# Other homes for the first operands of FFN-out in a one-core encoder layer

## The chip, the cores and the metric

The kernel runs on one core of a Trainium2 chip. The metric is the device time of one execution in microseconds; lower is better. The median of three runs before the change is 2306.59 us (2305.39 to 2307.46).

## What is computed

One layer of an encoder trunk on x of 1024 tokens by 1024 columns, in float32. It has three sub-layers, each between two RMS norms: a SwiGLU feed-forward block (FFN), a token mixing block (retention and neighbourhood attention), and a second FFN. The FFNs are what the change touches:

```python
def _swiglu(x, w_in, w_out):
    g, u = jnp.split(x @ w_in, 2, axis=-1)
    return (jax.nn.silu(g) * u) @ w_out
...
        h = _swiglu(_rms_norm(x, ffn1_pre_norm[l]), ffn1_w_in[l], ffn1_w_out[l])
        x = x + 0.5 * _rms_norm(h, ffn1_post_norm[l])
        m = _token_mixing(...)
        x = x + _rms_norm(m, mix_post_norm[l])
        h = _swiglu(_rms_norm(x, ffn2_pre_norm[l]), ffn2_w_in[l], ffn2_w_out[l])
        x = x + 0.5 * _rms_norm(h, ffn2_post_norm[l])
```

D_FF is 2816, that is 22 blocks of 128. "Layer 1" and "layer 2" below, and in the change's short description, are the first and the second FFN.

## The kernel before

**Products in three parts.** TensorE takes its operands in a reduced float format. So each float32 operand is split (`split`, L60 and L61): ScalarE casts it into a high part h, VectorE subtracts h and leaves a low part l. A product is then three matmuls, h·h, h·l and l·h (`mm3`, L87 to L89).

**Two-by-two blocks with seven products.** Both matrix products of an FFN are done as a Strassen-Winograd product: the left factor is kept as a11, a12, a22 and four sums s1 to s4, seven operands in place of eight blocks, and VectorE forms the sums of the right factor.

**FFN-in** (`ffn_in`, L404, and `Pairs.run`, L363) runs over 22 pairs, i = 0 to 21. A pair loads two raw weight tiles (tile wraw, three of 4 KB; all sizes here are per partition) and makes seven products in the order of the left operands a11, s2, a12, s3, s1, a22, s4. The left operands x (names a11h, a11l and so on, 14 tiles of 8 KB) stay in SBUF in pool a1 (layer 1) or a2 (layer 2). A pair's result is gated (SiLU at L414, product at L416) into a tile gt of 4 KB, of which there are three. After each second pair `LeftFactors` (L431) makes the left operand of FFN-out: GpSimd forms four sums (tile cmb, L441) from the halves of two gt tiles, and stores these and three unsummed halves to DRAM (tensors g0a.. and g0s.. in layer 1, g1a.. and g1s.. in layer 2). The stores are issued by GpSimd in the order of its list; a gt tile can be used anew when they have read it.

Before the 22 pairs, `Pairs.lead` (L330) makes the a11 and a12 products of the first six pairs in layer 1: three pairs stay in PSUM, three are saved in six tiles "lead" of 2 KB, which runs 3, 4 and 5 read at L376 (ScalarE) and L384 (VectorE). Beside the pairs `OutSums` (L508) prepares the right factor of FFN-out: for each of 11 column groups it loads four tiles tw (2 KB each, L517), makes four differences in place (L522) and stores them (tensors t).

**FFN-out** (`ffn_out`, L535) goes through 7 products x 11 blocks, 77 steps. A step takes a left block ("G operand") and a right block. `Blocks` (L446) loads the left block from DRAM into graw (L457, issued by SyncE), then splits it into gh and gl; the three are 2 KB each. The right block comes through wraw (L610, L614) and is split into wh and wl, of which there are eight each. A step has 12 matmuls, and operands are asked for three steps ahead. `Blocks` takes its pools in turn from a tuple of four: in layer 1 (g0, g0, g0, g1), so blocks 0, 1, 2 come from pool gl10 and block 3 from gl11, with three graw tiles in the first and one in the second; in layer 2 (g0, g1, g0, g1) with two each.

**Order and places.** Each engine works through its own list in order. The build makes the lists: it may put an instruction ahead of the program's order once its inputs and the place of its output are free. Pools are stacked in SBUF from two sides, left (upwards) and right (downwards). All pools here are opened with a rule by which a tile waits only for the tiles that had its bytes before, not for their whole pool. Between the end of the weight pool w and the right-hand edge there are 172 KB. Counted upwards from the end of w, in KB:

- layer 1, FFN-in: tw1 0 to 16; fin1 16 to 36 (two tiles each of c0 and c1 at 16 to 24, the three gt at 24 to 36); early 40 to 60 (four cmb, six lead); a1 60 to 172. Before it, norm1 had 0 to 28.
- layer 1, FFN-out: mid0 0 to 20; gl10 20 to 38 (graw 20 to 26, gh 26 to 32, gl 32 to 38); mid1 38 to 50; gl11 50 to 56; mid2 56 to 64; the rest on the right.
- layer 2, FFN-in: cmb2 0 to 8; tw2 8 to 24; fin2 24 to 44 (gt 32 to 44); a2 48 to 160; gs2 160 to 172.
- layer 2, FFN-out: out2 0 to 36; gl21 36 to 48; junk2 48 to 88; gl20 160 to 172.

Of the kernel before, what the change touches and what calls it, by code (L numbers as in the profile page):

```python
# [10 lines left out]
F32 = mybir.dt.float32  # L11
# [7 lines left out]
P = 128  # L19
# [216 lines left out]
class Winograd:  # L236
# [20 lines left out]
    def put(self, t, g, pt):  # L257
        c, nc = self.c, self.c.nc
        ts = slice((t % 4) * P, (t % 4 + 1) * P)
        if t < 4:  # L260
            c.split(*self.part(("a11", "a12")[g], ts), pt)
            return

        def tmp():
            return self.tmp.tile([P, 4, P], F32, tag="cmb", name="cmb", bufs=4)

        h1, l1 = [q.bitcast(F32) for q in self.part("a11", ts)]
        h2, l2 = [q.bitcast(F32) for q in self.part("a12", ts)]

        if g == 0:  # L270
            self.a21, self.s3 = tmp(), tmp()
            nc.scalar.copy(self.a21, pt)
            if self.spill is not None:
                c.store(self.spill[:, :, ts], self.a21)
            eng = nc.gpsimd if t in self.s3_on_pool else nc.vector
            eng.tensor_tensor(self.s3, h1, self.a21, ALU.subtract)
            eng.tensor_tensor(self.s3, self.s3, l1, ALU.add)
            return
        a21, s3 = self.a21, self.s3
        s1 = a21 if self.spill is None else tmp()  # L280
        c.split(*self.part("a22", ts), pt)
        nc.vector.tensor_tensor(s1, pt, a21, ALU.add)
        c.split(*self.part("s3", ts), s3)
        nc.vector.tensor_tensor(s3, pt, s3, ALU.subtract)
        c.split(*self.part("s1", ts), s1)
        c.split(*self.part("s2", ts), s3)
        nc.gpsimd.tensor_tensor(s3, h2, s3, ALU.subtract)  # L287
        nc.gpsimd.tensor_tensor(s3, s3, l2, ALU.add)  # L288
        return lambda: c.split(*self.part("s4", ts), s3, eng=nc.gpsimd)
# [9 lines left out]
class Pairs:  # L299
# [30 lines left out]
    def lead(self, save=None, between=(), on_pool=()):  # L330

        n = self.held + self.saved
        for i in (*range(self.held, n), *range(self.held)):
            if i in self.begun:
                continue
            g = self.c.raw(self.srcs[i][0])
            eng = self.c.nc.gpsimd if i in on_pool else None
            ps = [self.product("a11", g[:, :512], eng), self.product("a12", g[:, 512:], eng)]
            if between:
                f = between.pop(0)()  # L340
                if f is not None:
                    between.append(f)
            if i >= self.held:
                sb = [save(), save()]
                for a, b in zip(sb, ps):
                    for p, s in self.pieces(a):
                        self.c.nc.scalar.copy(p, b[:, s])
                ps = sb
            self.begun[i] = ps
# [54 lines left out]
def ffn_in(c, pairs, pool, put, sums):  # L404

    nc = c.nc
    for i in range(FT):
        gate = [pool.tile([P, 512], F32, tag=f"c{j}", name=f"c{j}", bufs=2) for j in range(2)]
        gt = pool.tile([P, S], F32, tag="gt", name="gt", bufs=3)
        up = gt[:, :512], gt[:, 512:]  # L410

        def done(j):
            if j < 2:
                nc.scalar.activation(gate[j], gate[j], AF.Silu)  # L414
            if j in (1, 2):
                e = nc.vector.tensor_tensor(up[j % 2], gate[j % 2], up[j % 2], ALU.mult)  # L416
                with c.tc.issue_after(e.ins):
                    sums(i, j)
        pairs.run(i, (*gate, *up).__getitem__, done)
        put(i, gt)  # L420
# [237 lines left out]
def stream(c, pool, src):  # L658

    def lhs(k, toks):  # L660
        n = len(toks) * P
        p0 = toks[0] * P
        raw = pool.tile([P, 384], F32, tag="graw", name="graw", bufs=2)
        h = pool.tile([P, 384], F32R, tag="gh", name="gh", bufs=3)
        l = pool.tile([P, 384], F32R, tag="gl", name="gl", bufs=3)
        c.nc.sync.dma_start(raw[:, :n], src(k)[:, p0:p0 + n])
        c.split(h[:, :n], l[:, :n], raw[:, :n])
        return {t: (h[:, j * P:(j + 1) * P], l[:, j * P:(j + 1) * P]) for j, t in enumerate(toks)}
    return lhs
# [340 lines left out]
def trunk_layer(ctx: ExitStack, tc, x, g1a, w1i, w1o, g1b, gma, wmt, wnv, wrv, logits, dtab, rope, bias,  # L1010
# [7 lines left out]
    c = Core(tc, const, wpool, psum, dram)  # L1018
# [4 lines left out]
    def dt(name, shape):  # L1023
        return dram.tile(shape, F32, name=name)

    gl = [{n: dt(f"g{i}{n}", [P, FT // 2 * 512]) for n in Winograd.NAMES} for i in range(2)]
    t1o, t2o = ([dt(f"t{i}{n}", [P, FT // 2 * 512]) for n in range(4)] for i in range(2))
# [9 lines left out]
    def rows(a):  # L1037
        return lambda t: a[t * P:(t + 1) * P, :]

    right, left = ExitStack(), ExitStack()  # L1040

    def pool(stack, name, side="left"):
        return stack.enter_context(tc.tile_pool(name=name, bufs=1, side=side, reuse_waits="tile"))
# [3 lines left out]
    early = pool(right, "early", "right")  # L1047
    wx = Winograd(c, (apool,) * 3, early, (14,) * 7)
    with tc.tile_pool(name="norm1", bufs=1, reuse_waits="tile") as ep:
        g = ep.tile([P, D], F32, tag="gpre", name="gpre", bufs=1)  # L1050
        nc.sync.dma_start(g, g1a)
        for t in range(TT):
            xt = ep.tile([P, D], F32, tag="epx", name="epx", bufs=3)
            nc.sync.dma_start(xt, x[t * P:(t + 1) * P, :])
            f = c.norm_T(xt, g, t, ep, wx.put)()
            if f is not None:
                f()
        fin = Pairs(c, wx, [(w1i[i], w1i[FT + i]) for i in LeftFactors.order], 3, 3)
        fin.lead(lambda: early.tile([P, 512], F32, tag="lead", name="lead", bufs=6), on_pool=(3, 4, 5, 0))
    with (tc.tile_pool(name="tw1", bufs=1, reuse_waits="tile") as tw,  # L1060
          tc.tile_pool(name="fin1", bufs=1, reuse_waits="tile") as fp):
        ffn_in(c, fin, fp, LeftFactors(c, early, gl[0]),
               OutSums(c, lambda: tw.tile([P, 512], F32, tag="tw", name="tw", bufs=8), w1o, t1o))
    right.close()

    x0pool = pool(right, "x0", "right")
# [2 lines left out]
    wx = Winograd(c, (x0pool, x1pool, None), None, (4, 4, 2, 8, 8, 8, 8), d["a21"])  # L1069
# [3 lines left out]
    q = [ep.tile([P, 4, 512], F32, tag="q", name="q", bufs=2) for _ in range(2)]  # L1073
# [4 lines left out]
    junk = [m0.tile([P, 512], F32, name=f"junk{u}") for u in range(2)]  # L1078
    g0 = pool(mid, "gl10")
    m1 = pool(mid, "mid1")  # L1080
    junk += [m1.tile([P, 512], F32, name=f"junk{u}") for u in range(2, 4)]
    g1, m2 = pool(mid, "gl11"), pool(mid, "mid2")
    rest = ffn_out(c, q, Blocks(c, (g0, g0, g0, g1), (3, 1)), junk,
                   lambda t: (m1, m2, ep, ep)[t // 2].tile([P, D], F32, tag="xs", name="xs", bufs=2 + t // 4 * 2),
                   w1o, t1o, gl[0], fo,
                   {n: (lambda j=j: ahead.update({j: c.load_w(wnv[j])})) for j, n in enumerate((65, 66))})
# [213 lines left out]
    cmb = pool(left, "cmb2")  # L1300
    wx = Winograd(c, (apool,) * 3, cmb, (14,) * 7)
    wx.s3_on_pool = (4, 5)
    with tc.tile_pool(name="ep2", bufs=1, reuse_waits="tile") as ep:
        rest = c.out_proj(KT, stream(c, gs, lambda k: d["m"][k]), lambda k: c.load_w(wmo[k]),
                          Ep(c, ep, gmb, g2a, False, rows(x1), rows(x2), wx.put))
        fin = Pairs(c, wx, [(w2i[i], w2i[FT + i]) for i in LeftFactors.order], 3, 1)

        def save():
            return [gs.tile([P, 384], F32, tag=n, name=n, bufs=3)[:, :256] for n in ("gh", "gl")]

        fin.lead(save, rest)
        for f in rest:
            f()


    tw = pool(left, "tw2")
# [3 lines left out]
    left.close()  # L1320
    a_stack.close()
    g_stack.close()
    g0 = pool(right, "gl20", "right")
    op = pool(left, "out2")
    q = [op.tile([P, 4, 512], F32, tag="q", name="q", bufs=4) for _ in range(4)]
    fo = Epilogue(c, op, g2b, None, rows(x2), rows(out), None)
    g1 = pool(left, "gl21")
    jp = pool(left, "junk2")
    junk = [jp.tile([P, 512], F32, name=f"junk{u}") for u in range(4)]
    ffn_out(c, q, Blocks(c, (g0, g1, g0, g1), (2, 2)), junk,  # L1330
# [81 lines left out]
```

## Time and profile before

| what | value |
|---|---|
| median of three runs | 2306.59 us |
| the profiled execution | 2306.69 us |
| its span on the core | 2304.8 us |
| granted TensorE clock, mean | 0.989 |
| ScalarE (ACT) busy | 1003.4 us, 44% |
| GpSimd (POOL) busy | 593.1 us, 26% |
| DMA | 422.63 MB, mean 183 GB/s |

The profile names the engines PE (TensorE matmul), PEld (its weight loads), DVE (VectorE), ACT (ScalarE), POOL (GpSimd) and SP (SyncE, which only issues DMAs). A row of the timeline gives start, duration, engine, line, operation, out<-in by the program's tile names, and how often; in brackets the idle time of the engine before it and what ended it. "wl<-wraw,wh" on DVE at L61 is the low part of a weight piece, "gh<-graw" on ACT at L60 the high part of a left block of FFN-out. Ends of matmuls are modelled: at full pace they start some 0.23 us apart and are shown 0.39 us long.

### The profile page before, as it was taken

The page shows a single profiled execution, that of the slowest core. Times are in us where ns is not written, and L with a number is a line of the kernel's source. Part 1 is how long each engine was busy: PE and PEld are TensorE (multiplying, and loading weights), DVE is VectorE, ACT ScalarE, POOL GpSimd, SP SyncE. Part 2 cuts the span into 40 slices and gives each one's busy share as a digit, 9 for nine tenths or more (in the row PEclk, how much of TensorE's full clock was granted, in tenths as well). Part 3 has the DMA queues.
Part 4 walks back from the last instruction along what each step waited for, and adds up shares of the span by engine and source line. Part 5 has one row for each costly group of instructions (what it writes and reads, how often), then busy time and mean ns, then how long its engine had stood idle before and what let it go on. Part 6 is the DMA issues. An engine that isn't in the chain of part 4 may idle for free.

```text
span 2304.8 us, 30361 instructions
## 1 busy us (share of the span) xinstructions
PE 2218.8 (96%) x10288; PEld 1839.6 (80%) x10288; DVE 1675.8 (73%) x2945; ACT 1003.4 (44%) x2102; POOL 593.1 (26%) x689
## 2 busy tenths in 40 slices
PE   6999999999998999999999999999799999998998
PEld 5788888778776877778888888887588888887886
DVE  7897777645778758869875688547897777774576
ACT  6333332244554322258885675225533322233453
POOL 5342423210124134411101222101534242421012
PEclk9999999999999999999999999999899999999999
DMA  5464545477654542257645577866555454546765
GB/s 177 153 205 147 178 144 176 153 231 227 207 192 142 178 165 96 110 185 238 220 161 178 163 222 235 291 213 204 173 172 187 151 173 146 174 138 213 233 199 185
DMA packets 163675, 422.63 MB, mean 183 GB/s; under 512 B 19712, under 2 KB 47488, under 8 KB 163456
## 3 DMA queue, kind: packets, MB, share of 16 engines
q1 hardware_dynamic: 130080, 310.04, 42.4%
q0 software_dynamic: 33440, 110.65, 12.4%
q8 instruction: 81, 1.33, 0.2%
q14 instruction: 74, 0.61, 0.1%
HBM read 301.60 MB, written 123.21 MB: 184 GB/s over the span
## 4 chain that ended last, share of the span: by engine, by line
PE 80%; DVE 11%; issue 3%; POOL 3%; DMA 1%; ACT 1%; SPq 0%; POOLq 0%; DVEq 0%; ACTq 0%
PE ps L89 25%; PE ps L87 24%; PE ps L88 24%; DVE wl L61 2%; PE pt L89 1%; PE pt L87 1%; PE pt L88 1%; POOL rstd L97 1%; PE ps L725 1%; PE pt L744 1%; POOL cmb L287 1%; DVE tmp L117 1%; DVE t L378 1%; POOL cmb L288 1%; DVE xs L493 1%
## 5 line engine op out<-in xcount | busy, mean ns | idle before, releaser
L61 DVE TENSOR_TENSOR wl<-wraw,wh 128x512 fp32r<-128x512 f32 x662 | 468.9, 728 | 80.4 <-ACT wh L60 79.4
L60 ACT CAST wh<-wraw 128x512 fp32r<-128x512 f32 x670 | 390.3, 618 | 218.2 <-PE ps L88 71.2
L87 PE MATMUL ps<-wh,gh 128*128 128x512 f32 x612 | 241.5, 396 | 19.2 <-ACT gh L60 18.1
L61 DVE TENSOR_TENSOR gl<-graw,gh 128x512 fp32r<-128x512 f32 (+2 forms) x178 | 124.3, 699 | 173.8 <-ACT gh L60 173.6
L88 PE MATMUL ps<-wl,gh 128*128 128x512 f32 x612 | 241.2, 395 | 2.1 <-DVE wl L61 2.1
L89 PE MATMUL ps<-wh,gl 128*128 128x512 f32 x612 | 240.1, 395 | 0.8 <-DVE gl L61 0.5
L60 ACT CAST gh<-graw 128x512 fp32r<-128x512 f32 (+2 forms) x178 | 107.1, 602 | 226.6 <-PE ps L88 87.4
L414 ACT ACTIVATE c<-c 128x512 f32<-128x512 f32 x88 | 55.7, 633 | 283.1 <-DVE c L384 198.5
L87 PEld LDWEIGHTS ps<-wh,gh 128*128 128x128 f32 x612 | 116.4, 190 | 45.9 <-ACT gh L60 19.7
L89 PEld LDWEIGHTS ps<-wh,gl 128*128 128x128 f32 x612 | 116.4, 191 | 28.2 <-DVE gl L61 4.0
L88 PEld LDWEIGHTS ps<-wl,gh 128*128 128x128 f32 x612 | 116.6, 191 | 26.8 <-DVE wl L61 3.2
L483 POOL TENSOR_TENSOR q<-q,gain 128x512 f32<-128x512 f32 x22 | 33.6, 1546 | 357.7 <-ACT ps L482 343.4
L60 ACT CAST wh<-t 128x512 fp32r<-128x512 f32 x58 | 36.1, 622 | 202.6 <-DVE t L378 184.5
L89 PE MATMUL ps<-a12h,wl 128*128 128x512 f32 x280 | 110.4, 394 | 3.7 <-DVE wl L61 3.7
L87 PE MATMUL ps<-a11h,wh 128*128 128x512 f32 x280 | 112.4, 401 | 1.4 <-ACT wh L60 0.7
L89 PE MATMUL ps<-a11h,wl 128*128 128x512 f32 x280 | 110.9, 396 | 0.7 <-DVE wl L61 0.7
L87 PE MATMUL ps<-a12h,wh 128*128 128x512 f32 x280 | 111.1, 397 | 0.0
L88 PE MATMUL ps<-a11l,wh 128*128 128x512 f32 x280 | 111.0, 397 | 0.0
L88 PE MATMUL ps<-a12l,wh 128*128 128x512 f32 x280 | 109.8, 392 | 0.0
L87 PE MATMUL ps<-a22h,wh 128*128 128x512 f32 x280 | 109.8, 392 | 0.0
L89 PE MATMUL ps<-a22h,wl 128*128 128x512 f32 x280 | 109.1, 390 | 0.0
L88 PE MATMUL ps<-a22l,wh 128*128 128x512 f32 x280 | 109.0, 389 | 0.0
(354 smaller groups left out, 5975.6 us busy)
## 6 DMA issues: line engine op xcount, KB each, us to landing
wraw<-in_dram SPq DMA_DIRECT2D x243, 512.0 KB, 4.4
tw<-in_dram SPq DMA_DIRECT2D x88, 256.0 KB, 3.3
t<-tw POOLq DMA_DIRECT2D x88, 256.0 KB, 4.2
wraw<-t SPq DMA_DIRECT2D x40, 512.0 KB, 3.6
g0s<-cmb POOLq DMA_DIRECT2D x44, 256.0 KB, 4.2
graw<-g0s SPq DMA_DIRECT2D x44, 256.0 KB, 2.8
g1s<-cmb POOLq DMA_DIRECT2D x44, 256.0 KB, 4.2
graw<-g1s SPq DMA_DIRECT2D x44, 256.0 KB, 2.7
```

What stands on the lines that cost most here:

```text
L60: nc.scalar.copy(h, src)
L61: (eng or nc.vector).tensor_tensor(l, src, hf, ALU.subtract)
L87: mm(ps, a[0], b[0], start=start, stop=False)
L88: mm(ps, a[0], b[1], start=False, stop=False)
L89: mm(ps, a[1], b[0], start=False, stop=stop)
L97: self.nc.gpsimd.tensor_tensor(r[:, :n], ms, self.mhalf[:, :n], ALU.pow)
L117: nc.vector.scalar_tensor_tensor(xn[:, bs], x[:, bs], r[:, 0:1], gain[:, bs], op0=ALU.mult, op1=ALU.mult)
L287: nc.gpsimd.tensor_tensor(s3, h2, s3, ALU.subtract)
L288: nc.gpsimd.tensor_tensor(s3, s3, l2, ALU.add)
L378: tt(t2, b22, t1, ALU.subtract)
L414: nc.scalar.activation(gate[j], gate[j], AF.Silu)
L483: (eng or c.nc.gpsimd).tensor_tensor(h if out is None else out, h, self.post[:, b * 512:(b + 1) * 512], ALU.mult)
```

## The change

In layer 1 the pool tw1 is gone: the tw tiles are taken from the same tag as the saved leads, "lead", which has eight tiles in place of six. So FFN-in of layer 1 has only fin1 on the left side, now at 0 to 20 KB, and the pool early grows to 24 KB (36 to 60). `Blocks` of layer 1 gets two graw tiles in each pool in place of three and one; gl10 is then 16 KB (20 to 36), mid1 36 to 48, gl11 48 to 56.

In layer 2 a loop calls `wx.op` for the seven left operands of FFN-in in the reverse of the order in which a pair uses them, before the products that fill them; and gl21 moves to the right side, below gl20, at 148 to 160 KB, so that junk2 begins at 36.

```diff
         fin = Pairs(c, wx, [(w1i[i], w1i[FT + i]) for i in LeftFactors.order], 3, 3)
-        fin.lead(lambda: early.tile([P, 512], F32, tag="lead", name="lead", bufs=6), on_pool=(3, 4, 5, 0))
-    with (tc.tile_pool(name="tw1", bufs=1, reuse_waits="tile") as tw,
-          tc.tile_pool(name="fin1", bufs=1, reuse_waits="tile") as fp):
-        ffn_in(c, fin, fp, LeftFactors(c, early, gl[0]),
-               OutSums(c, lambda: tw.tile([P, 512], F32, tag="tw", name="tw", bufs=8), w1o, t1o))
+
+
+        def lead():
+            return early.tile([P, 512], F32, tag="lead", name="lead", bufs=8)
+
+        fin.lead(lead, on_pool=(3, 4, 5, 0))
+    with tc.tile_pool(name="fin1", bufs=1, reuse_waits="tile") as fp:
+        ffn_in(c, fin, fp, LeftFactors(c, early, gl[0]), OutSums(c, lead, w1o, t1o))
     right.close()
...
-    rest = ffn_out(c, q, Blocks(c, (g0, g0, g0, g1), (3, 1)), junk,
+    rest = ffn_out(c, q, Blocks(c, (g0, g0, g0, g1), (2, 2)), junk,
...
     wx.s3_on_pool = (4, 5)
+    for n in ("s4", "a22", "s1", "s3", "s2", "a12", "a11"):
+        wx.op(n)
...
-    g0 = pool(right, "gl20", "right")
+    g0, g1 = pool(right, "gl20", "right"), pool(right, "gl21", "right")
     op = pool(left, "out2")
     q = [op.tile([P, 4, 512], F32, tag="q", name="q", bufs=4) for _ in range(4)]
     fo = Epilogue(c, op, g2b, None, rows(x2), rows(out), None)
-    g1 = pool(left, "gl21")
     jp = pool(left, "junk2")
```

## The prediction

> **What bounds the kernel now.** I read the page first (busy shares, slices, chain), then windows of 10 us around the two thin places of the slices, then the timeline there.
>
> ```profile
> PE 2218.8 (96%) x10288; PEld 1839.6 (80%) x10288; DVE 1675.8 (73%) x2945; ACT 1003.4 (44%) x2102; POOL 593.1 (26%) x689
> PE   6999999999998999999999999999799999998998
> PE 80%; DVE 11%; issue 3%; POOL 3%; DMA 1%; ACT 1%; SPq 0%; POOLq 0%; DVEq 0%; ACTq 0%
> ```
>
> TensorE is busy 96% of the span and carries 80% of the chain, so only its idle time and its slow time can be won. Two idle places lie where FFN-in hands over to FFN-out; call them joint 1 (layer 1) and joint 2 (layer 2). Columns: stretch, then busy us of PE, PEld, DVE, ACT, POOL, granted clock, DMA share, GB/s.
>
> ```profile
> 450.00:460.00 10.00, 6.29 (x28) 4.88 (x26) 6.97 (x11) 2.50 (x4) 2.79 (x4) 1.00 0.42 134
> 460.00:470.00 10.00, 3.84 (x9) 3.02 (x10) 1.33 (x2) 1.24 (x2) 6.80 (x9) 0.53 0.67 246
> 470.00:480.00 10.00, 10.00 (x43) 8.20 (x43) 5.33 (x9) 5.30 (x10) 0.00 (x0) 0.96 0.84 270
> 2070.00:2080.00 10.00, 8.98 (x40) 7.12 (x38) 7.53 (x12) 3.64 (x6) 2.80 (x4) 1.00 0.43 137
> 2080.00:2090.00 10.00, 3.88 (x9) 3.06 (x10) 3.46 (x4) 1.24 (x2) 7.24 (x9) 0.60 0.81 268
> 2090.00:2100.00 10.00, 10.00 (x41) 8.08 (x41) 3.88 (x6) 3.46 (x7) 0.00 (x0) 0.89 0.48 152
> ```
>
> Joint 1 in the timeline (start, duration, engine, line, tiles, and in brackets the idle time before it with its releaser):
>
> ```profile
> 455.90 0.39 PE L89 MATMUL ps<-s4h,wl 128*128 128x512 f32 x1
> 461.11 0.56 POOL L67 DMA_DIRECT2D t<-tw  x1
> 462.89 0.56 POOL L67 DMA_DIRECT2D g0a<-gt  x1
> 465.25 0.32 SPq L457 DMA_DIRECT2D graw<-g0a  x1
> 465.49 0.62 ACT L60 CAST gh<-graw 128x512 fp32r<-128x512 f32 x1 [8.72 <-DMA g0a<-gt]
> 466.16 0.80 PE L87 MATMUL ps<-wh,gh 128*128 128x512 f32 x1 [9.87 <-ACT gh L60]
> 471.19 0.39 PE L87 MATMUL ps<-wh,gh 128*128 128x512 f32 x1
> ```
>
> FFN-in's last matmul ends at 456.29. The first cast into gh (L60) stands still until the store of the last gated tile has read it: POOL issues that store only at 462.89, behind its sums. So the home of gh is a gt tile, and the pool sizes say the same: counted from the end of the weight pool, fin1's gt fills 24 to 36 KB, gl10's gh 26 to 32. PE loses 9.87 us. Then it runs slowly: the block's 12 matmuls take 466.16 to 471.19, 5.03 us. A block at full pace is the step between these two loads, 2.72 us:
>
> ```profile
> 478.02 0.32 SPq L457 DMA_DIRECT2D graw<-g0a  x1
> 480.74 0.32 SPq L457 DMA_DIRECT2D graw<-g0s  x1
> ```
>
> That is 2.31 us more. Joint 2 differs: block 0 runs at once, block 1 waits.
>
> ```profile
> 2076.10 0.39 PE L87 MATMUL ps<-wh,gh 128*128 128x512 f32 x1
> 2081.62 0.32 SPq L457 DMA_DIRECT2D graw<-g1a  x1
> 2085.45 1.25 ACT L60 CAST gh<-graw 128x512 fp32r<-128x512 f32 x2 [5.52 <-DMA graw<-g1a]
> 2086.12 0.79 PE L87 MATMUL ps<-wh,gh 128*128 128x512 f32 x1 [7.14 <-ACT gh L60]
> 2092.23 0.40 PE L89 MATMUL ps<-wh,gl 128*128 128x512 f32 x1
> ```
>
> ```profile
> SPq L457 <- POOL cmb L441: 0.7, 1, 0.7
> ```
>
> Block 1's load (pool gl21, 36 to 48 KB) lies on fin2's gt (32 to 44 KB); SP's last wait before it is for POOL's sum L441, which reads gt. PE idles 7.14 us; the 14 starts from 2086.12 to 2092.23 take 6.11 us where 14/12 x 2.72 = 3.17 would do: 2.94 more.
>
> **The change, part by part.**
>
> *Joint 1.* fin1 moves down to 0 to 20 KB; gl10 (graw 2, gh 3, gl 3 tiles of 2 KB) takes 20 to 36 KB, and the enlarged early pool begins at 36 of the 172 KB that are free. Nothing that FFN-in uses is left under blocks 0, 1 and 2. What then holds them? Only their stores and the engines' queues. Layer 2 already shows such operands:
>
> ```profile
> 1756.26 0.33 SPq L457 DMA_DIRECT2D graw<-g1a  x1
> 1760.61 0.62 ACT L60 CAST gh<-graw 128x512 fp32r<-128x512 f32 x1 [4.68 <-DMA graw<-g1a]
> 1761.26 0.69 DVE L61 TENSOR_TENSOR gl<-graw,gh 128x512 fp32r<-128x512 f32 x1 [2.34 <-ACT gh L60]
> 1760.00:1770.00 10.00, 10.00 (x46) 8.29 (x45) 7.62 (x13) 3.46 (x7) 0.00 (x0) 1.00 0.25 84
> ```
>
> This one is loaded some 320 us ahead, and the row of 2076.10 above has no idle time in brackets: PE goes from FFN-in to block 0 without a gap. So joint 1 should lose its 9.87 us, and without idle time also the slow 2.31: 12.18 us. What is late next is block 3 (pool gl11, 48 to 56 KB), now on the lead tiles, in which w_out's sums end. PE wants it at 456.29 + 3 x 2.72 = 464.45. The last of those stores is issued at 461.11 and lands 2.3 us later:
>
> ```profile
> t<-tw POOLq DMA_DIRECT2D x1, 256.0 KB, 2.3
> DMA to landing us min/median/max: 2.5/2.8/4.4
> ```
>
> That is 463.4. If gh or gl of block 3 lies there, cast and difference (0.62 + 0.69) end at 464.7: at most 0.3 lost. If graw does (one of eight tiles), a load of 2.8 (second row, graw in FFN-out) comes first: 467.5, 3.1 us lost. I take 0.
>
> *Two graw tiles for three of four blocks* (was 3 and 1). A tile is wanted again after two blocks, 5.44 us; cast, difference and load need 0.62 + 0.69 + 2.8 = 4.1, with the longest load 5.7. Casts run more than two blocks ahead of PE, which covers the 0.3. Cost 0; above, 0.3 if that cover goes.
>
> *Joint 2.* gl21 goes to the right side, 148 to 160 KB, on top of FFN-in's operands a2. There are two readings of the new loop over op(). If tiles take their place when first written, as the q tiles of the built program do (q[2], written before q[1], stands in the place that is given out earlier), the layout stays and gl21 lies on a11l and a12h. If the loop reverses it, gl21 lies on s4l and a22h. Last uses in the last pair:
>
> ```profile
> L89 PE MATMUL ps<-a12h,wl x8: 389/389/389, 2043.9 to 2065.0; 128*128 128x512 f32 x8
> L88 PE MATMUL ps<-s4l,wh x8: 389/389/389, 2054.6 to 2075.6; 128*128 128x512 f32 x8
> ```
>
> On a12h the loads start at 2065.4 and all is there 11 us early. On s4l the cast starts at 2076.0; with DVE's tail before it gl is done by 2078 to 2079.5, wanted at 2076.10 + 2.72 = 2078.82: 0 to 0.7 lost. I take 0: gain 7.14 + 2.94 = 10.08. Blocks 0 and 2 keep their pool.
>
> *The front of layer 1.* The w_out tiles tw lose their own 16 KB and share eight with the six saved leads. Two are free at once; the rest come free only as runs 3 to 5 read their leads:
>
> ```profile
> L376 ACT COPY c<-lead x3: 621/622/623, 99.2 to 128.2; 128x512 f32<-128x512 f32 x3
> L384 DVE TENSOR_TENSOR c<-lead,c x3: 676/693/1070, 117.1 to 145.3; 128x512 f32<-128x512 f32 x3
> L522 DVE TENSOR_TENSOR tw<-tw x16: 677/682/1186, 96.6 to 192.2; 128x512 f32<-128x512 f32 x16
> DMA to landing us min/median/max: 2.4/4.1/6.4
> 130.00:140.00 10.00, 9.84 (x44) 7.83 (x43) 9.97 (x13) 4.57 (x8) 7.25 (x9) 1.00 0.75 270
> ```
>
> Six of the first eight loads and their subtractions (L522, 0.68 each) move 20 to 45 us later, into a stretch where DVE is full (9.97 of 10) and PE just fed (9.84). The work is the same. Two loads may also run ahead into the first 10 us; 0.52 MB at 270 GB/s (the last row) are 1.9 us if all of it delays the start, 0 if none. PE can gain 0.16 there at most. I take half, +0.9; ends -0.2 and, if DVE waits in full, the slow rival below.
>
> *Sum.* -12.18 - 10.08 + 0.9 = -21.4 us. The profiled execution took 2306.69 us (span 2304.8), the median is 2306.59: **2285 us**. Work behind the joints follows them in fixed order with PE full, so I let the shift carry to the end.
>
> [...]
>
> **The rivals.**
>
> *Block 3's graw waits for the last tw store* (10%): -21.4 + 3.1 = 2288; with a slow restart as in joint 1, 2291. For it: one tile in eight. Against: a tile freed one pair earlier serves as well.
>
> *The order of the queues stays* (8%): block 0's home is free, but SP still loads it after the last w_out load.
>
> ```profile
> 458.03 7.53 SPq L457 DMA_DIRECT2D graw<-g0a  x2
> graw<-g0a SPq DMA_DIRECT2D x1, 256.0 KB, 4.1
> ```
>
> 458.03 + 4.1 + 0.62 = 462.8: 6.5 idle plus 2.3 slow remain, 2285 + 8.8 = 2294. Against it: the load at 1756.
>
> *The reversed layout binds joint 2* (5%): +0.7, and 2.9 if PE restarts slowly: up to 2289.
>
> *The front pays* (11%): the two extra loads in full and some waits of DVE for tw, +3 to +10: 2287 to 2295.
>
> *The change doesn't do what it says* (5%): other tiles in use lie under the new homes, both gaps stay: 2307 (2297 if one stays). Against: the sizes above.
>
> *Slower* (4%): DVE's list waits for moved data. Three early gl at 2.34 each are 7.0; six tw loads waited for in full, 4.1 each, are 24.6; 31.6 - 22.3 = +9, 2316. It decides once DVE waits over 22.3 us in a stretch where PE has no reserve. Against it: in layer 2 the 2.34 cost PE nothing (10.00 of 10). [...] The row of 1761.26 shows DVE standing for a cast.
>
> **How the numbers follow.** The forecast, 2285 (2282 to 2288), has 57%. The range 2281 to 2294.5 takes in the block 3 and layout rivals, the queue rival, most of the front and PE's small gain at the start; some 2 in 10 lie outside. A measurement tells 0.2%, 4.6 us, from no change: faster 91%, same 5%, slower 4%.
>
> **What would show it.** Right: graw, gh, gl of blocks 0 to 2 appear during FFN-in of layer 1; PE shows no idle time over 1 us and a clock of 1.00 at both joints; PE stays at 9.8 or more of 10 from 90 to 150. Wrong: a gh cast released by a g0a or t store at joint 1, idle time of PE before run 6, or a gap that moves to block 3.

## The result, and the profile after

The changed kernel takes **2317.99 us** (median of 5 runs, 2314.03 to 2319.92) beside 2306.59 for the kernel before (5 runs, 2305.39 to 2309.05): a ratio of 1.0047, 95% interval 1.0036 to 1.0059. It is slower by 11.4 us where 21.6 us less were forecast. The profiled execution took 2318.16 us, its span is 2316.4.

The page of the changed kernel: busy shares, PE in 40 slices, the chain by engine.

```profile
PE 2228.1 (96%) x10288; PEld 1843.5 (80%) x10288; DVE 1683.6 (73%) x2945; ACT 1003.5 (43%) x2102; POOL 592.7 (26%) x689
PE   6989999989999999999999999999799999999998
PE 79%; DVE 10%; issue 4%; POOL 3%; DMA 2%; ACT 2%; POOLq 0%; DVEq 0%; SPq 0%; ACTq 0%
```

The slice of joint 2, the fourth from the right, is 9 now and was 8. But the third (116 to 174 us, the front of layer 1) and the ninth (463 to 521, joint 1) are 8 and were 9. To see what each part of the program took, cut the span at the last matmul of FFN-in in each layer. Timeline of the changed kernel:

```profile
473.50 0.39 PE L89 MATMUL ps<-s4h,wl 128*128 128x512 f32 x1
2093.47 0.39 PE L89 MATMUL ps<-s4h,wl 128*128 128x512 f32 x1
```

Before, they start at 455.90 and 2075.87. So the **front** (start to the last of these matmuls in layer 1, "the last s4 matmul" below) takes 17.60 us more; from there to the end of FFN-in in layer 2, where joint 1 lies, 1619.97 us both times, no change; from there to the end of the span, where joint 2 lies, 2316.4 - 2093.47 = 222.9 in place of 228.9. 17.6 + 0 - 6.0 = 11.6, which is the whole difference of the spans (2316.4 - 2304.8). The three parts are read one by one.

**The front.** Windows of the changed kernel (columns as in the prediction):

```profile
120.00:130.00 10.00, 6.40 (x25) 4.44 (x23) 7.07 (x12) 2.05 (x4) 2.17 (x4) 0.86 0.70 216
130.00:140.00 10.00, 9.63 (x34) 7.59 (x34) 9.20 (x12) 2.12 (x4) 6.71 (x7) 0.79 0.72 243
140.00:150.00 10.00, 6.14 (x25) 4.35 (x24) 6.06 (x9) 1.77 (x3) 3.96 (x7) 1.00 0.92 309
150.00:160.00 10.00, 7.86 (x20) 5.50 (x21) 7.59 (x14) 3.31 (x6) 1.62 (x3) 0.66 0.41 139
```

PE is fed only 6.1 to 9.6 of 10 us, at a clock of 0.66 to 1.00; before it was busy 9.84 or more of 10 in each of them, at 1.00. The waits between 100 and 165 us (engine, line, waited for: us in total, times, longest):

```profile
PE ps L87 <- ACT wh L60: 6.7, 3, 3.3
PE ps L89 <- DVE wl L61: 3.6, 4, 1.9
DVE lead L522 <- DMA lead<-in_dram: 5.8, 3, 3.7
DVE wraw L377 <- DMA wraw<-in_dram: 3.6, 2, 3.1
SPq L517 <- DMA t<-lead: 15.8, 8, 3.4
```

PE stands for 6.7 + 3.6 = 10.3 us; the other 7.3 of the 17.6, by difference, go with the matmuls at the slow pace behind these stops (the clock is 0.50 from 127.30 to 134.12 and from 151.18 to 158.02 us). DVE stands 5.8 us for w_out data that has not come, and that data waits in SP's list for a lead place. The timeline shows the lists:

```profile
116.71 0.62 ACT L376 COPY c<-lead 128x512 f32<-128x512 f32 x1 [3.15 <-DVE gt L416]
117.25 0.69 DVE L384 TENSOR_TENSOR c<-lead,c 128x512 f32<-128x512 f32 x1
117.36 0.33 SPq L517 DMA_DIRECT2D lead<-in_dram  x1
121.64 0.69 DVE L522 TENSOR_TENSOR lead<-lead 128x512 f32<-128x512 f32 x1 [3.70 <-DMA lead<-in_dram]
...
120.36 0.33 SPq L457 DMA_DIRECT2D graw<-g0a  x1
120.79 20.52 SPq L517 DMA_DIRECT2D lead<-in_dram  x11
143.08 0.97 SPq L71 DMA_DIRECT2D wraw<-in_dram  x2
```

ScalarE's copy frees a lead place at 117.33, and SP issues the load into it at 117.36. DVE is done with L384 at 117.94 and then stands 3.70 us, until this load has landed. The place that L384 itself frees is loaded only at 120.79: in SP's list an early load of a left block (120.36) stands ahead, which waits for that block's store. SP spends 20.5 us on 11 w_out loads and issues the next raw weights only behind them, at 143.08; before, it issued raw weights at 125 and 127 too. By then it is DVE that frees the raw tile for this load last, by a difference (L61) that starts at 142.37. DVE's 3.1 us for raw weights follow from the late load.

**Joint 1.** Blocks 0 to 2 run without a gap, the first at 473.72. Then:

```profile
479.22 0.56 POOL L67 DMA_DIRECT2D t<-lead  x1
484.08 1.85 SPq L457 DMA_DIRECT2D graw<-g0a  x3
491.16 0.62 ACT L60 CAST gh<-graw 128x512 fp32r<-128x512 f32 x1 [8.17 <-DMA graw<-g0a]
491.83 0.79 PE L87 MATMUL ps<-wh,gh 128*128 128x512 f32 x1 [9.79 <-ACT gh L60]
```

How long the three loads of the second row took to land, and the windows over this stretch:

```profile
DMA to landing us min/median/max: 5.9/6.6/6.7
```

```profile
480.00:490.00 10.00, 2.04 (x10) 1.35 (x8) 4.66 (x4) 1.42 (x3) 4.96 (x7) 0.78 0.86 283
490.00:500.00 10.00, 8.17 (x28) 6.53 (x29) 2.04 (x4) 2.47 (x5) 0.00 (x0) 0.70 0.33 94
```

The gap has moved to block 3 and is as long as before, 9.79 us for 9.87. In the built program the last w_out tile lies at 48 KB, as block 3's first graw tile does; its store goes out at 479.22 and lands 3.3 us later, at 482.5. Block 3's load is the second of the three that SP issues from 484.08, behind a load for a later block; the three land 5.9 to 6.7 us after their issue, among the stores of the last G operands, with the DMA engines busy 0.86 of the time. PE wanted block 3 at 473.89 + 3 x 2.72 = 482.05. So the 9.8 us are some 0.5 until the store has landed, 1.9 in SP's list, 6.6 for the load and 0.8 for the cast. The clock of 0.70 behind the gap is the slow pace once more.

**Joint 2.** Block 0 again starts at once, at 2093.69.

```profile
2076.78 13.92 SPq L610 DMA_DIRECT2D wraw<-in_dram  x5
2091.26 0.85 SPq L457 DMA_DIRECT2D graw<-g1a  x2
...
2096.39 1.66 ACT L60 CAST gh<-graw 128x512 fp32r<-128x512 f32 x3 [2.04 <-PE ps L88]
2097.58 0.50 PE L87 MATMUL ps<-wh,gh 128*128 128x512 f32 x1 [1.00 <-ACT gh L60]
2099.81 0.91 PE L89 MATMUL ps<-wh,gl 128*128 128x512 f32 x2 [1.04 <-DVE gl L61]
```

The window behind it, and the last use of a12h (span 2000 to 2095 us):

```profile
2100.00:2110.00 10.00, 10.00 (x38) 8.09 (x38) 6.51 (x7) 3.43 (x6) 4.88 (x7) 0.83 0.93 311
```

```profile
L89 PE MATMUL ps<-a12h,wl x20: 389/389/389, 2004.4 to 2082.6; 128*128 128x512 f32 x20
```

Block 1's home on a11l and a12h is free early: the last matmul that reads a12h starts at 2082.6. But its load stands in SP's list behind the first loads of FFN-out's weights and goes out at 2091.26. It lands 3.6 us later, at 2094.9; cast and difference (0.62 + 0.69) could have followed by 2096.2, and PE is done with block 0 at 2096.4. So the load is still just in time, and the lists of ACT and DVE are not. On ACT the first of the three casts from 2096.39 is not block 1's: it waits 2.04 us for PE to be done with block 0, whose place it takes, so it is block 4's, listed ahead. On DVE the differences follow in the same order. PE idles 1.00 + 1.04 us in place of 7.14, and some slow pace remains (0.83).

### The profile page after: what moved, and what is told of

Same layout as the page of the kernel before. It is cut to its first block, busy times and chain, and to the rows that moved or that the text cites. A ratio compares the mean times of both kernels' runs of the same rounds, so it can differ in the third digit from the quotient of the medians.

```text
span 2316.4 us, 30350 instructions
## 1 busy us (share of the span) xinstructions
PE 2228.1 (96%) x10288; PEld 1843.5 (80%) x10288; DVE 1683.6 (73%) x2945; ACT 1003.5 (43%) x2102; POOL 592.7 (26%) x689
## 3 DMA queue, kind: packets, MB, share of 16 engines
q0 software_dynamic: 33440, 110.65, 12.4%
## 4 chain that ended last, share of the span: by engine, by line
PE 79%; DVE 10%; issue 4%; POOL 3%; DMA 2%; ACT 2%; POOLq 0%; DVEq 0%; SPq 0%; ACTq 0%
PE ps L89 24%; PE ps L87 24%; PE ps L88 24%; DVE wl L61 2%; PE pt L89 1%; PE pt L88 1%; PE pt L87 1%; DMA wraw<-in_dram 1%; PE ps L725 1%; PE pt L744 1%; POOL rstd L97 1%; POOL cmb L287 1%; POOL cmb L288 1%; DVE xs L493 1%; DVE gl L61 1%
## 5 line engine op out<-in xcount | busy, mean ns | idle before, releaser
L61 DVE TENSOR_TENSOR wl<-wraw,wh 128x512 fp32r<-128x512 f32 x662 | 472.9, 734 | 81.0 <-ACT wh L60 80.1
L61 DVE TENSOR_TENSOR gl<-graw,gh 128x512 fp32r<-128x512 f32 (+2 forms) x178 | 128.4, 722 | 164.2 <-ACT gh L60 162.7
```

The source lines that it names most:

```text
L61: (eng or nc.vector).tensor_tensor(l, src, hf, ALU.subtract)
```

## The experiments

Medians and ratios stand beside runs of the kernel before on the same chip: 2305.51 us for the first four, 2307.20 for the next four, 2305.63 for the last. The table cuts each profiled span as above. Parts that no edit touches differ by up to 1.2 us from the kernel before, and by up to 2.1 from one another; that is the table's grain.

| kernel | front | to FFN-in's end, layer 2 | rest | front against before | joint 1 | joint 2 |
|---|---|---|---|---|---|---|
| before | 455.90 | 1619.97 | 228.9 | | | |
| changed | 473.50 | 1619.97 | 222.9 | +17.6 | 0.0 | -6.0 |
| sharing alone | 468.23 | 1619.44 | 228.2 | +12.3 | -0.5 | -0.8 |
| layer 2 alone | 455.93 | 1620.28 | 221.3 | 0.0 | +0.3 | -7.6 |
| block 3 moved | 473.44 | 1609.39 | 222.9 | +17.5 | -10.6 | -6.0 |
| w_out by POOL's queue | 471.47 | 1620.14 | 221.6 | +15.6 | +0.2 | -7.3 |
| leads' own home | 455.27 | 1608.89 | 229.6 | -0.6 | -11.1 | +0.7 |
| layer 2, three ahead | 456.19 | 1620.82 | 218.7 | +0.3 | +0.9 | -10.3 |
| both layouts | 456.35 | 1609.56 | 218.7 | +0.5 | -10.4 | -10.3 |
| block 3 moved, sums late | 458.51 | 1609.20 | 222.9 | +2.6 | -10.8 | -6.1 |
| sharing alone, sums late | 455.45 | 1618.74 | 228.1 | -0.5 | -1.2 | -0.8 |

### The sharing alone

```diff
-        fin.lead(lambda: early.tile([P, 512], F32, tag="lead", name="lead", bufs=6), on_pool=(3, 4, 5, 0))
+        def lead():
+            return early.tile([P, 512], F32, tag="lead", name="lead", bufs=8)
+
+        fin.lead(lead, on_pool=(3, 4, 5, 0))
...
+        tw.tile([P, 4096], F32, name="pad")
-               OutSums(c, lambda: tw.tile([P, 512], F32, tag="tw", name="tw", bufs=8), w1o, t1o))
+               OutSums(c, lead, w1o, t1o))
```

> The kernel before, with one part of the change alone: the w_out tiles of layer 1 take turns on the eight lead places. A pad of 16 KB stands where tw1 stood, so FFN-out's operands, both pools of them, keep the homes that they have before. Theory 1 (the sharing itself costs the front of FFN-in: tw loads wait for lead places and hold up SP's list): the last s4 matmul of layer 1 starts near 473.5 us in place of 455.9, and the time is 2306.6 + 17.6 = about 2324. Rival (the early casts and loads of FFN-out's operands cost the front): the last s4 matmul stays near 455.9 and the time within 2 us of 2306.6.

Measured: 2318.07 us, ratio 1.0054 (1.0041 to 1.0068). The sharing costs by itself, 12.3 us of the front, and the rival falls; but the size is not the full 17.6. The 5.3 us that are missing come with the early blocks (their loads in SP's list, their casts and differences on ACT and DVE), in company with the sharing. DVE's waits from 100 to 165 us are like those of the changed kernel:

```profile
DVE lead L522 <- DMA lead<-in_dram: 5.2, 3, 3.3
DVE wraw L377 <- DMA wraw<-in_dram: 4.7, 1, 4.7
```

### Layer 2's part alone

```diff
-    g0 = pool(right, "gl20", "right")
+    g0, g1 = pool(right, "gl20", "right"), pool(right, "gl21", "right")
...
-    g1 = pool(left, "gl21")
```

> The kernel before, with layer 2's part alone: gl21 is opened on the right beside gl20, and the loop that names the operands in reverse is left out. Theory 1 (the part is worth what the changed kernel shows at joint 2, and the loop moves no place): the first block of FFN-out starts without a gap, gaps of about 1 us remain before the second, and the time is 2306.6 - 6.05 = about 2300.5. Rival (the loop does the work): the gap of 7.14 us before FFN-out's first block remains, 2306.6. The forecast's own step would give 2306.6 - 10.1 = 2296.5.

Measured: 2300.00 us, ratio 0.9977 (0.9968 to 0.9987). Without the loop the part is worth what it is worth with it, so the new home does the work. (In the built programs the addresses of a2's tiles are the same with and without the loop; a trace does not show addresses.) The gap of 7.14 us that the rival names stood before the second block, not the first. PE's two stops are those of the changed kernel, to the hundredth:

```profile
2080.32 0.50 PE L87 MATMUL ps<-wh,gh 128*128 128x512 f32 x1 [1.00 <-ACT gh L60]
2082.55 0.73 PE L89 MATMUL ps<-wh,gl 128*128 128x512 f32 x2 [1.04 <-DVE gl L61]
```

The window over them:

```profile
2080.00:2090.00 10.00, 8.64 (x37) 6.82 (x38) 8.64 (x8) 3.76 (x8) 7.63 (x10) 1.00 0.80 249
```

The slow pace behind them is missing here, though (clock 1.00), which makes the 1.6 us between -7.6 and -6.0; the last section sets the two runs side by side.

### Block 3 moved

```diff
-    g1, m2 = pool(mid, "gl11"), pool(mid, "mid2")
+    m2 = pool(mid, "mid2")
+    pad = pool(mid, "pad1")
+    pad.tile([P, 1024], F32, name="pad")
+    g1 = pool(mid, "gl11")
```

> The changed kernel, with the pool of block 3 (gl11) opened behind mid2 and a pad of 4 KB, so that it lies on a11h, which FFN-in is done with after its fifth product, and not on the last w_out tile. Theory 1 (block 3's first raw waits for the store of the last w_out tile, and this makes the gap of 9.79 us): the gap before block 3 goes, the slow go behind it too (2 to 2.4 us), and the time is 2318.0 - 12 = about 2306; the front still costs 17.6. Rival (the lists put block 3's loads late wherever it lies): the gap stays within 2 us of 9.79 and the time near 2318.

Measured: 2306.62 us, ratio 1.0001 (0.9992 to 1.0010). The home was the cause: on a11h, block 3 comes in time and joint 1 closes, while the front still costs 17.5. Windows of this run over joint 1:

```profile
470.00:480.00 10.00, 10.00 (x45) 8.26 (x45) 8.38 (x12) 4.46 (x8) 5.22 (x6) 1.00 0.71 231
480.00:490.00 10.00, 10.00 (x46) 8.27 (x45) 7.77 (x9) 3.65 (x7) 4.92 (x7) 1.00 0.85 286
```

### The first w_out loads by POOL's queue

```diff
-            self.c.nc.sync.dma_start(t, src[:, k * 512:(k + 1) * 512])
+            (self.c.nc.gpsimd if self.dst is self.other and k < 4 else self.c.nc.sync).dma_start(t, src[:, k * 512:(k + 1) * 512])
...
+        ffn_in(c, fin, fp, LeftFactors(c, early, gl[0]), OutSums(c, lead, w1o, t1o, t1o))
```

> The changed kernel, with the loads of w_out for the first four groups of layer 1 issued by POOL's queue in place of SP's. Theory 1 (SP's list, filled with w_out loads that wait for a lead place, holds up the raw loads of the weights behind it, and this is most of the front's 17.6 us): the raw loads of FFN-in go out by 140 us as before, the last s4 matmul starts near 460, and the time is about 2318.0 - 13 = 2305. Rival (DVE's in-order list waits for w_out data that arrives late, and casts of weights stand behind it): DVE's waits for w_out loads, 5.8 us between 118 and 133, stay or grow, and the last s4 matmul starts at 470 or later, 2315 to 2325.

Measured: 2316.03 us, ratio 1.0044 (1.0030 to 1.0057); the last s4 matmul starts at 471.47. The rival holds. SP's list is clear of w_out loads up to 154 us, and the raw weights still go out at 114.9 and then only at 138.1 us. The waits from 100 to 165 us say why:

```profile
DVE lead L522 <- DMA lead<-in_dram: 5.9, 3, 3.5
...
SPq L71 <- DVE wl L61: 46.0, 8, 18.1
```

SP now waits up to 18.1 us for DVE to free a raw tile, and DVE stands as long for w_out data as before. SP's crowded list was a second place where the same delay showed, not its source; 2 of the 17.6 us hung on it. (GpSimd's list also holds the stores that free the places, and the loads in it now wait 4.9 us for stores, so this run is no clean measure of what SP's list alone costs.)

### A home of their own for the leads

```diff
-        fin.lead(lambda: early.tile([P, 512], F32, tag="lead", name="lead", bufs=6), on_pool=(3, 4, 5, 0))
+        leads = pool(right, "lead1", "right")
+        fin.lead(lambda: leads.tile([P, 512], F32, tag="lead", name="lead", bufs=6), on_pool=(3, 4, 5, 0))
...
-    g0 = pool(mid, "gl10")
     m1 = pool(mid, "mid1")
...
-    g1, m2 = pool(mid, "gl11"), pool(mid, "mid2")
-    rest = ffn_out(c, q, Blocks(c, (g0, g0, g0, g1), (3, 1)), junk,
+    pad = pool(mid, "pad1")
+    pad.tile([P, 1024], F32, name="pad")
+    g0, m2, g1 = pool(mid, "gl10"), pool(mid, "mid2"), pool(mid, "gl11")
+    rest = ffn_out(c, q, Blocks(c, (g0, g0, g0, g1), (2, 2)), junk,
```

> The kernel before in layer 2; in layer 1 the w_out tiles keep their own pool, and the six lead tiles get a pool of their own that lies beside the 4 KB which stand empty in FFN-in. FFN-out's first three operands (16 KB) take these two places, which no instruction touches after the sixth run of FFN-in, and block 3 lies on a11h. Theory 1 (the homes are worth what the gap says, and only the sharing, with casts that come in the crowded stretch up to 160 us, made the front dear): no gap before FFN-out's first four blocks, no slow go behind them, the last s4 matmul stays near 455.9, and the time is 2305.5 - 12.2 = about 2293. Rival (early loads and casts of G operands cost the front wherever they are put, up to the 17.6 - 12.3 = 5.3 us that the changed kernel lost beyond the sharing): about 2298.

Measured: 2295.15 us, ratio 0.9943 (0.9923 to 0.9963): -12.1 us from 2307.20, where theory 1 said -12.2. Windows over joint 1:

```profile
450.00:460.00 10.00, 10.00 (x45) 8.28 (x45) 8.13 (x13) 4.17 (x7) 3.42 (x4) 1.00 0.62 205
460.00:470.00 10.00, 10.00 (x46) 8.26 (x44) 8.47 (x9) 4.26 (x8) 6.72 (x9) 1.00 0.75 238
```

The casts of the early blocks in the timeline:

```profile
149.46 1.14 ACT L60 CAST gh<-graw 128x512 fp32r<-128x512 f32 x2
164.28 0.62 ACT L60 CAST gh<-graw 128x512 fp32r<-128x512 f32 x1 [9.11 <-DMA graw<-g0a]
```

The same three blocks come early here too, but from 149 us on, and w_out keeps its places. The front is untouched. The joint can be priced more closely at the first matmul of FFN-out's 41st block: before, it starts at 577.31, 121.41 us behind the last s4 matmul; here at 564.29, 109.02 us behind it. That is 12.4 us; the 11.1 of the table also holds what the later parts, which no edit touches, gained or lost. Two graw tiles in place of three cost nothing, as forecast.

### Layer 2 with three blocks ahead

```diff
+    pool(g_stack, "pad2", "right").tile([P, 1024], F32, name="pad")
     a_stack = ExitStack()
...
-    g0 = pool(right, "gl20", "right")
+    g0, g1 = pool(right, "gl20", "right"), pool(right, "gl21", "right")
...
-    g1 = pool(left, "gl21")
...
-    ffn_out(c, q, Blocks(c, (g0, g1, g0, g1), (2, 2)), junk,
+    ffn_out(c, q, Blocks(c, (g0, g0, g0, g1), (2, 2)), junk,
```

> The kernel before, with layer 2 alone changed in another way: a pad of 4 KB beside gs2, so that gl20 has 16 KB and holds the first three blocks of every four, on places that FFN-in does not touch at its end; gl21 (8 KB) lies on a11l. Theory 1 (what joint 2 still lost was block 1, whose load and casts stand in the lists behind work of FFN-in's end): no gap at all at joint 2, no slow go, and the time is 2305.5 - 10.1 = about 2295.5. Rival (the lists put the casts of blocks 1 and 2 late as well, or the slow go comes whatever the gaps): gaps of about 1 us or a slow go remain, and the time stays near that of layer 2's part alone, 2300.

Measured: 2296.81 us, ratio 0.9957 (0.9942 to 0.9972): -10.4 us. Joint 2 is closed, at full clock:

```profile
2070.00:2080.00 10.00, 10.00 (x46) 8.29 (x45) 7.53 (x12) 2.58 (x5) 1.66 (x3) 1.00 0.56 192
2080.00:2090.00 10.00, 10.00 (x46) 8.29 (x45) 9.42 (x9) 5.02 (x9) 8.47 (x10) 1.00 0.71 225
```

So the rest of joint 2 was block 1's late place in the lists. By the rows of the changed kernel these are ACT's and DVE's, since the load had landed in time; no run moves them one by one.

### Both layouts

The edits of the last two together.

> The two other layouts together: the lead tiles' own pool in layer 1 and the pad in layer 2. Theory 1 (the two joints are independent): the gains add, 2305.5 - 12.2 - 10.1 = about 2283. Rival (each layout keeps the loss that its own rival names, 5 us in the front of layer 1 and 4.5 us at joint 2): about 2293.

Measured: **2285.46 us**, ratio 0.9904 (0.9887 to 0.9920): -21.7 us, the gains add. This version beats both kernels. Its page:

```profile
PE 2216.7 (97%) x10288; PEld 1838.9 (80%) x10288; DVE 1682.5 (74%) x2945; ACT 1001.9 (44%) x2102; POOL 593.4 (26%) x689
PE   6999999999998999999999999999899999999998
```

### The w_out sums late

The kernel with block 3 moved, and in `OutSums.__call__`, for layer 1 only:

```diff
-        if j == 1 and (i == 0 or i % 2 == 1 and i < FT - 2):
-            self.load((i + 1) // 2)
-        for n in ((0, 2), (1, 3))[j - 1] if i == 1 else ():
-            self.sub(0, n)
-        if i > 1:
-            self.sub(i // 2, (0, 2, 1, 3)[i % 2 * 2 + j - 1])
+        if i == 5 and j == 1:
+            self.load(0)
+        m = (i - 6) * 2 + j
+        while i > 5 and self.n < 44 * m // 32:
+            if self.n % 4 == 2 and self.n < 40:
+                self.load(self.n // 4 + 1)
+            self.sub(self.n // 4, (0, 2, 1, 3)[self.n % 4])
+            self.n += 1
```

> The changed kernel with block 3 on a11h, and with the w_out sums of layer 1 begun in run 6, when the copies of runs 3 to 5 have freed their lead places, in place of run 1; the 44 sums are spread over the last 16 runs. Theory 1 (the sharing costs because the first sums stand in DVE's list at places where their tiles still wait for a lead place): the 12.3 us of the sharing go, the last s4 matmul starts at 456 to 462, and the time is 2306.6 - 12.3 = about 2294. Rival (the sharing costs through the stores that each tile's next load waits for, whenever the sums begin, or the denser sums hold up DVE as much): the last s4 matmul starts at 470 or later, 2304 to 2312.

Measured: 2292.17 us, ratio 0.9937 (0.9922 to 0.9952). The sharing stays and its cost goes: the last s4 matmul starts at 458.51, 2.6 us late in place of 17.5. DVE no longer waits for w_out data between 100 and 165 us; it stands for early casts almost alone (7.8 us), and has room for it: it is busy 51.2 of the 60 us from 100 to 160, and was 58.7 before. The waits, then a window:

```profile
DVE gl L61 <- ACT gh L60: 7.8, 2, 4.2
```

```profile
120.00:130.00 10.00, 9.00 (x39) 6.83 (x38) 7.79 (x13) 4.13 (x7) 0.54 (x1) 1.00 0.14 51
```

### The sharing with late sums, without early casts

The edit of the first experiment and the late sums of the last, without its moved block 3.

> The kernel of the first run (the shared lead places alone, old homes for FFN-out's operands) with the w_out sums of layer 1 begun in run 6 and spread over the last 16 runs, so without casts of G operands in FFN-in's front. It completes a table of two by two: shared places with early sums cost the front 12.3 us without and 17.6 us with early casts, late sums 2.6 us with them. Theory 1 (the early casts cost little by themselves and add to a list of DVE that is already behind): the last s4 matmul starts 2 to 3 us before that of the run with casts, at 455.5 to 456.5, and the time is within 2 us of the kernel before, some 2306. Rival (the 2.6 us are those of the sharing and the denser sums, and the early casts cost nothing once the sums are late): the last s4 matmul starts at 458 to 459, about 2309.

Measured: 2305.29 us, ratio 0.9999 (0.9989 to 1.0008); last s4 matmul at 455.45. Theory 1 holds, and the table is complete:

| front, us | without early casts | with early casts |
|---|---|---|
| shared places, sums from run 1 | +12.3 | +17.6 |
| shared places, sums from run 6 | -0.5 | +2.6 |

The early blocks cost 3.1 us where DVE has room and 5.3 where its list is already behind. In the leads' own home, where they come later, they cost nothing that shows. Casts and loads were not tried apart: from 100 to 165 us SP, too, stands 12.6 us in the changed kernel, and 6.3 with late sums, for the stores that early loads wait for.

## Why the prediction was wrong

*What bounds the kernel* and *the price of the two joints* were right. Closed at last, both are worth what the rows of before said: 12.18 forecast for joint 1, 12.1 measured by the medians and 12.4 at the 41st block; 10.08 and 10.4 for joint 2. So the slow pace costs about what those rows gave, 2.31 and 2.94 us. The kernel with both takes 2285.46 us where 2285 was forecast, but that is another kernel. What failed is that this change closes them, and at what cost. Two of the prediction's own signs of being wrong came: idle time of PE before run 6, and a gap that moves to block 3. One reading was off without harm: joint 1 is no thin place of the slices (it falls on the border of two that show 9); only the windows show it.

*The front of layer 1* (forecast +0.9, upper end +1.9): mis-sized, +17.6. The step held that the sums "move 20 to 45 us later", that "the work is the same", and priced the extra loads. But it read the warning rows, DVE 9.97 of 10 and PE just fed, and then let DVE's list wait at no cost. The first sums stand in DVE's list close behind the instructions that free their places; between the two lie a copy or a store, SP's turn and a load. DVE waits 5.8 us for that, with the casts' low parts and the sums of the weights queued behind. The slower rival named this mechanism at 4% and gave 2316; that its time was near was luck, for the terms were not: it had 31.6 us of waits against the full 22.3 of gain, and the runs show 17.6 against 6.0.

*Other kernels separate the work from the wait.* Before, and with the leads' own home, DVE is busy 58.7 and 59.5 of the 60 us from 100 to 160 and never waits for w_out: no cost. With late sums it has less to do there (51.2) and waits 7.8 us for early casts: 2.6. Where the sums stay in the crowded stretch and wait for data 5.2 to 5.8 us, the cost is 12.3 and 17.6. So it is neither the work nor the wait alone; how a wait of 5.8 us grows to 17.6 was not followed step by step.

*Joint 1* (forecast -12.18): 0. Blocks 0 to 2 came early, as the step said; block 3 took over the gap. The prediction had this rival at 10% with 3.1 us, 6 with a slow restart. Its mechanism was right and its price for the gap was a third: it let the load start as soon as the store had landed and take 2.8 us. The store landed at 482.5, the load waited its turn in SP's list until 484.4 and then took 6.6 us among the last stores. The argument "one tile in eight" was the wrong kind: the tile follows from the order in which places are given out, and that could have been counted.

*Joint 2* (forecast -10.08): -6.0. The step asked when block 1's home is free (2082.6, early enough) and not where its load and casts stand in the lists. "All is there 11 us early" is what failed (by its own rows, 2065.4 + 2.8 + 0.62 + 0.69 = 2069.5 against 2078.82, it should have said 9): the load went out at 2091.26 and landed 1.5 us before block 1 was due, and its cast and difference then stood behind those of block 4. The reading that the loop moves no place fits the run without the loop.

*The queue order* was asked of joint 1 (rival at 8%) from block 0's row alone. There it did not come true. At block 3 SP's list cost 1.9 us, and at block 1 of layer 2 the lists of ACT and DVE cost the two stops.

## What to carry to other kernels

A gap is worth its idle time plus the slow pace behind it (here 9.87 + 2.31 and 7.14 + 2.94 us), and that can be read off; whether a new home closes it depends on every operand that comes due within the gap's length, and for each one on its place in the lists, not on when the bytes are free. Saving space by letting two uses share places puts waits into the lists of all who use them (here 5.2 to 5.9 us of DVE's for w_out data): look at the engine that must wait, and where its list is full and TensorE has no reserve, move the work past the crowded stretch or find space that is dead there (here the leads' own places).

## What the hardware showed beside this

The same two stops at joint 2, 1.00 and 1.04 us before the same two instructions, have different sequels. In the changed kernel:

```profile
2100.51 0.63 PE L87 MATMUL ps<-wh,gh 128*128 128x512 f32 x1
2100.94 0.63 PE L88 MATMUL ps<-wl,gh 128*128 128x512 f32 x1
```

In the run of layer 2's part alone, as long behind the second stop:

```profile
2083.36 0.40 PE L88 MATMUL ps<-wl,gh 128*128 128x512 f32 x1
2083.59 0.39 PE L89 MATMUL ps<-wh,gl 128*128 128x512 f32 x1
```

Starts 0.43 us apart, near half pace, at a clock of 0.83 in the window; and 0.23 apart, at 1.00. The traces tell more when they are cut at the steps of the granted clock. In the changed kernel it is 0.50 from 2100.20 to 2103.61 us, 3.41 us long, and 1.00 before and behind. In the traces of this kernel and of the kernel before, the steps of the clock (21 and 15) lie whole multiples of 3.413 us apart, counted from 45.38 and from 44.18 us. The stretch of the same length just before has PE busy 1.58 of 3.41 us, since both stops fall into it. Cutting the other runs in the same raster, counted on from their own steps, gives:

| kernel | PE busy of 3.41 us, in the stretches with the stops | clock behind | joint 2 |
|---|---|---|---|
| changed | 1.58 | 0.50 for 3.41 us | -6.0 |
| block 3 moved | 1.42 | 0.50 for 3.41 us | -6.0 |
| block 3 moved, sums late | 1.45 | 0.50 for 3.41 us | -6.1 |
| layer 2 alone | 2.13, then 2.66 | 1.00 | -7.6 |
| w_out by POOL's queue | 2.41, then 2.37 | 1.00 | -7.3 |

The stops are the same five times. In the three runs where one stretch holds nearly all of both (1.83 to 1.99 us of idle time), half pace followed; in the two where the border parts them (1.28 us at most in one stretch), it did not. No single stop here is longer than 1.04 us, and PE was busy 0.42 to 0.46 of the time in the stretches that half pace followed. That share alone does not decide: from 1635.99 to 1639.41 us of the changed kernel PE was busy 0.44 of the time, and the clock stayed 1.00 up to 1642.82. What does was not shown.

The duration of a load differed with the place where it fell: 256 KB of graw took a median of 2.8 us in FFN-out before, and 5.9 to 6.7 at joint 1 of the changed kernel, just behind the stores of the last G operands, when the DMA engines were busy 0.86 of the time. That share alone does not explain it: before, with 0.80 from 490 to 500 us, no load of graw issued there took more than 3.1.
